# Queries, keys and values kept in DRAM in the layout of their later loads, and the left half of the first output tile moved up to the last GELU

## The chip, the cores and the metric

The kernel runs on one core of one Trainium2 chip. The metric is the device time of one execution in microseconds. Five engines run their own instruction streams: TensorE (PE) multiplies, VectorE (DVE) and ScalarE (ACT) do the elementwise work, GpSimd (POOL) some of it, and the SyncE queue (SP) issues nearly all transfers. Sixteen DMA engines carry the transfers.

## What is computed

One pre-norm layer on x of shape 2048 x 1024 in float32: a token mixer with eight attention heads of width 64 (with forget gates) beside a gated MLP over chunks of 128 positions, one output projection, a dense SwiGLU layer, and a last RMS norm.

```
xn = rms_norm(x, mix_norm_g)
q, k, v, f_logit, z = split(xn @ w_in)                  # 512, 512, 512, 8, 1024 columns
c = cumsum(log_sigmoid(f_logit + b_f))
attn = softmax(q k^T / 8 + c[t] - c[s], s <= t) @ v     # 8 heads of width 64
zu, zv = split(gelu(z)); sgu = zu * (w_s @ layer_norm(zv) + b_s)
x = x + concat(rms_norm(attn), rms_norm(sgu)) @ w_out
gate, up = split(rms_norm(x) @ w_gate_up)
x = x + (silu(gate) * up) @ w_down
out = rms_norm(x)
```

## The kernel before

All products are done in a float32 form with fewer mantissa bits (`F32R`). To keep the accuracy each operand is split into a rounded half ("hi", written h) and the rest ("lo", written l), and a product is the sum of three: hi by hi, hi by lo, lo by hi. A product of 128 x 512 outputs over 1024 inputs is thus 24 matmuls.

**Stage 1, to about 340 us: projections.** The 2048 positions are taken in four chunks of 512 (`c` in line 485). For each chunk the loop at line 508 makes eight products, four for the queries and four for the keys; each holds two heads of 64 rows on the 128 partitions. VectorE scales the result into `ql` (line 521), ScalarE rounds it into `qh` (523 or 528), VectorE leaves the rest in `ql` (524 or 529), and both go to DRAM, 256 KB each (lines 525, 526, 530, 531): `QH`, `QL`, `KH`, `KL`, one tensor of [128, 512] per pair of heads and chunk. `qh` and `ql` are two tiles deep (line 518: pool `p1`, bufs=2), so the tiles of product n+2 are free when the stores of product n have landed. Four products for the values follow (line 557; in the first chunk they come earlier), which `v_close` (419) splits and stores in `VD`. Between the products, `between` (403) lets side work run: the next chunk's loads and splits (`Chunk.steps`), the forget gates (`forget_rows`, which stores f in `FD` and loads it again at line 292 with the block index in front: 4 blocks by 8 heads by 128), and `max_stream` (359), which reads keys and queries back (tiles `A` and `D`) to find the maximum of each row of logits.

All of these transfers stand in one SyncE queue and are issued in order.

**Stage 2, about 340 to 900 us: attention and gates.** `load_keys` (611) brings a block of keys and values: hi and lo of the keys into the two halves of tile `C`, hi again into `D`, and the values in three transfers into `V` (hi, lo, and one column of lo), beside a column of ones that was set once (600 to 604). `prep` (645) does the same for queries (`A`, `B`). `qk` (669) and `pv_of` (706) do the attention steps; ScalarE's exponentials (680) stand between them. In their gaps `z_proj` (815) makes the gates' products, with two transfers of 512 KB for each tile `xz`, and ends each group of four with one GELU over 128 x 2048 (835).

**Output tiles, from about 896 us.** `out_prep` (984) makes the operands of an output tile, `out_tiles` (1060) does its two products (left and right half, `fh` 0 and 1), 24 matmuls each, at line 1079, and adds them to the tile of x. From about 1105 us the SwiGLU layer follows, to the end.

The order on each engine is not that of the code: a scheduler in the build places instructions, and a change in one place moves others by a few places.

Of the kernel before, what the change touches and what calls it, by code (L numbers as in the profile page):

```python
# [15 lines left out]
P = 128  # L16
S = 2048
D = 1024
KT = D // P
# [59 lines left out]
def trunk(ctx: ExitStack, tc: tile.TileContext, x, x_t, mix_g, w_in, b_f, ln_g, ln_b, w_st, b_st, on_g, w_out,  # L79
# [279 lines left out]
    def max_stream(units, pl, ps, pp, nd, ahead):  # L359

        jobs = [(h, j, s) for h, j in units for s in range(j + 1)]
        As, Ds = {}, {}

        def get(n):
            if n < len(jobs):
                h, j, s = jobs[n]
                pr, o = h // 2, (h % 2) * DH
                if s == 0:
                    A = As[h, j] = T(pl, [66, CH], F32R, "A", bufs=2)
                    ldr(A[0:64], QH[pr][j][o : o + DH])  # L370
                    ldr(A[64:66], CR[0:2])
                Dt = Ds[n] = T(pl, [66, CH], F32R, "D", bufs=nd)
                ldr(Dt[0:64], KH[pr][s][o : o + DH])
                ldr(Dt[64:66].rearrange("r (b t) -> r b t", t=P), aug_rows(h, s, slice(2 * j, 2 * j + 2)))

        def turn():
            max_rows(pp, T(ps, [P, 4, P], F32, "mx_ps" if ps is ps2_[0] else "tp", **kw), *late)

        late, kw = None, {"bufs": NMX} if ps is ps2_[0] else {}
        for n in range(ahead):  # L380
            get(n)
        if ps is ps2_[0]:
            yield
        for n, (h, j, s) in enumerate(jobs):
            get(n + ahead)
            if s == 0:
                mx = T(pp, [P, 4, 4], F32, "mx")
            for a in range(4):
                one_max(ps, pp, a, j, s, As[h, j][:, a * P : (a + 1) * P], Ds[n], mx)
                yield  # L390
                if a == 2 and late is not None:
                    turn()
                    late = None
            if s == j:
                late = (h, j, max_split(pp, j, mx))
        yield
        turn()
        yield
# [20 lines left out]
    def v_close(pm, xc, tt):  # L419
        v = T(p1, [P, H, P], F32R, "v") if xc.c else T(p1, [P, H, P], F32R, "xh", bufs=4)  # L420
# [64 lines left out]
    for c in range(NCH):  # L485
# [22 lines left out]
        for which, w in ((0, wq), (1, wk)):  # L508
            for pr in range(4):
# [86 lines left out]

# [3 lines left out]
    with tc.high_priority():  # L600
        for v in vt[:2]:
            nc.vector.memset(f(v[:, :, DH : DH + 1]), 1.0)
    for v in vt[2:]:
        nc.gpsimd.memset(f(v[:, :, DH : DH + 1]), 1.0)
# [6 lines left out]
    def load_keys(h, s, i):  # L611
# [4 lines left out]
        ldr(C[0:64], KH[pr][s][o : o + DH])  # L616
        ldr(C[64:128], KL[pr][s][o : o + DH])
        ldr(Dt[0:64], KH[pr][s][o : o + DH])
        ldr(Dt[64:74].rearrange("r (b t) -> r b t", t=P), aug_rows(h, s, slice(0, 10)))
        vd = VD[s][h].rearrange("(b p) d -> p b d", p=P)  # L620
# [24 lines left out]
    def prep(h, j, res):  # L645
        pr, o = h // 2, (h % 2) * DH
        A = T(p2k, [74, CH], F32R, "A")
        ldr(A[0:64], QH[pr][j][o : o + DH])
        ldr(A[64:72], CR[8 * j : 8 * j + 8])
        B = T(p2k, [P, CH], F32R, "B")  # L650
        ldr(B[0:64], QL[pr][j][o : o + DH])
        ldr(B[64:128], QH[pr][j][o : o + DH])
# [331 lines left out]
    def out_prep(t, o, space=None):  # L984
# [23 lines left out]
        def inputs():  # L1008
            o["x"] = x_tile(t)
            ld(o["x"], x[t * P : (t + 1) * P, :])  # L1010
# [14 lines left out]
        if space is not None:  # L1025
            o["ahead"] = True
# [32 lines left out]

    def out_tiles():  # L1060
        groups = [[0, 1]] + [[t] for t in range(2, NB - 2)] + [[NB - 2, NB - 1]]
        gens = first + [out_prep(t, o[t]) for t in range(2, NB)]
        for its in groups:
# [7 lines left out]
            for fh in range(2):  # L1071
                for t in its:
                    ps = E["bank"]()
                    n = 0
                    for k in (4, 5, 6, 7, 0, 1, 2, 3):
                        wh, wl = (a[:, k % 4, :] for a in o[t]["s"][k // 4])
                        rh, rl = (a[:, k, :] for a in WO[fh])
                        for a, b in ((wh, rh), (wh, rl), (wl, rh)):
                            nc.tensor.matmul(ps, a, b, start=n == 0, stop=n == 3 * KT - 1)
                            n += 1  # L1080
# [41 lines left out]
    for n in range(len(steps) + DEPTH):  # L1122
# [25 lines left out]
        if z_done == z_total and not wg:  # L1148
            while next(zg) == "on":
                pass  # L1150
            for _ in lm:
                pass
            while not all(o[t].get("ahead") for t in range(2)):
                for g in first:
                    next(g)
# [429 lines left out]
```

## Time and profile before

| what | value |
|---|---|
| median of three runs | 2421.05 us (2418.85 to 2423.35) |
| the profiled execution's own time | 2428.99 us |
| its span in the profile | 2427.1 us |
| PE busy | 2369.9 us, 98% |
| VectorE, ScalarE, GpSimd busy | 69%, 44%, 25% |
| DMA | 404920 packets, 372.09 MB, mean 153 GB/s |
| HBM read, written | 249.09 MB, 120.92 MB |

The profile is of one execution. Busy shares are means over stages that are limited by different things; a matmul's busy time overlaps that of the next, so that the pitch from start to start, not the mean duration, is what a matmul costs. "DMA share" is the mean busy share of the 16 DMA engines: a transfer that keeps two of them busy shows as 0.13, one that keeps all of them busy as 1.00. "PEclk" is the share of full speed at which TensorE's clock was granted.

### The profile page before, as it was taken

How to read it: one execution, taken by the hardware profiler on the slowest of the kernel's cores; microseconds unless marked ns; L12 is line 12 of the kernel's file. 1: busy time of each engine (PE TensorE's matmuls, PEld its weight loads, DVE VectorE, ACT ScalarE, POOL GpSimd, SP SyncE). 2: the span in 40 equal slices, each digit the busy share in tenths (PEclk: the TensorE clock that was granted, in tenths of full speed). 3: DMA queues.
4: the chain of work that ended last, by engine and by line, in shares of the span. 5: the costliest groups of instructions: out<-in, count | busy, mean ns of one | idle time of the engine just before them, and what ended most of it. 6: DMA issues, size and time to landing. Idle time of an engine off the chain costs nothing. (4 is left out here: it accounts for less than half of the span.)

```text
span 2427.1 us, 31390 instructions
## 1 busy us (share of the span) xinstructions
PE 2369.9 (98%) x10585; PEld 1902.6 (78%) x10585; DVE 1667.1 (69%) x2710; ACT 1059.1 (44%) x1770; POOL 610.3 (25%) x662
## 2 busy tenths in 40 slices
PE   9999999999999989999999999999999999999997
PEld 7778777777777767787888888788888878888886
DVE  6557677878887666466656555965655596686878
ACT  5322136767777765344333232433323242332333
POOL 1000001121111221221323232332323244363451
PEclk9999999999999989999999999999999999999998
DMA  8856466666686664675432322433232245455443
GB/s 277 298 168 205 127 198 174 172 168 156 156 222 185 183 181 135 200 220 167 122 96 84 91 70 87 139 87 95 76 90 70 87 139 181 166 182 201 160 170 146
DMA packets 404920, 372.09 MB, mean 153 GB/s; under 512 B 72660, under 2 KB 326420, under 8 KB 402712
## 3 DMA queue, kind: packets, MB, share of 16 engines
q1 hardware_dynamic: 399512, 355.33, 48.4%
q0 software_dynamic: 2880, 10.49, 1.5%
q10 hardware_dynamic: 2368, 4.26, 0.5%
q8 instruction: 85, 1.39, 0.2%
q14 instruction: 75, 0.61, 0.1%
HBM read 249.09 MB, written 120.92 MB: 152 GB/s over the span
## 5 line engine op out<-in xcount | busy, mean ns | idle before, releaser
L111 ACT CAST wh<-raw 128x512 fp32r<-128x512 f32 (+2 forms) x496 | 304.3, 620 | 743.9 <-PE pp L1523 620.5
L114 DVE TENSOR_TENSOR wl<-raw,wh 128x512 fp32r<-128x512 f32 (+2 forms) x496 | 371.9, 760 | 87.7 <-ACT wh L111 87.5
L1523 PE MATMUL pp<-wl,wh 128*128 128x512 f32 x1056 | 326.5, 390 | 1.8 <-ACT u L1279 1.0
L1523 PE MATMUL pp<-wh,wh 128*128 128x512 f32 x1056 | 326.1, 390 | 0.0
L1213 POOL TENSOR_TENSOR raw<-raw 128x512 f32<-128x512 f32 (+1 forms) x124 | 169.6, 1369 | 509.7 <-DMA raw<-in_w_gu_dram 351.4
L114 DVE TENSOR_TENSOR Pl<-Pt,Ph 128x512 fp32r<-128x512 f32 (+1 forms) x320 | 195.2, 615 | 87.1 <-ACT Ph L111 82.2
L1523 PEld LDWEIGHTS pp<-wl,wh 128*128 128x128 f32 x1056 | 198.0, 188 | 44.7 <-ACT u L1279 1.4
L1523 PEld LDWEIGHTS pp<-wh,wh 128*128 128x128 f32 x1056 | 198.3, 188 | 41.9
L680 ACT ACTIVATE Pt<-st 128x512 f32<-128x512 f32 (+1 forms) x320 | 169.9, 534 | 136.5 <-PE st L678 132.5
L1523 PE MATMUL pp<-wl,wl 128*128 128x512 f32 x528 | 206.2, 391 | 0.7 <-DVE wl L114 0.7
L1523 PE MATMUL pp<-wh,wl 128*128 128x512 f32 x528 | 206.1, 390 | 0.4 <-DVE wl L114 0.4
L827 PE MATMUL z<-wh,xz 128*128 128x512 f32 x512 | 197.8, 404 | 7.2 <-DMA xz<-XS 7.2
L111 ACT CAST Ph<-Pt 128x512 fp32r<-128x512 f32 (+1 forms) x320 | 176.1, 556 | 27.7 <-PE pv L712 9.1
L1213 DVE TENSOR_TENSOR raw<-raw,raw 128x512 f32<-128x512 f32 (+1 forms) x112 | 133.2, 1192 | 78.9 <-POOL raw L1213 75.5
L335 DVE TENSOR_REDUCE mx<-mx_ps 128x1 f32<-128x512 f32 x192 | 129.8, 683 | 30.5 <-PE mx_ps L333 29.6
L690 POOL TENSOR_SCALAR_AFFINE_SELECT Ph<-Ph 128x128 fp32r<-128x128 f32 x128 | 49.7, 388 | 360.9 <-DVE Pl L114 283.0
L677 PE MATMUL st<-A,D 74*128 74x512 f32 (+1 forms) x320 | 120.4, 376 | 7.2 <-ACT Pt L680 7.0
L710 PE MATMUL pv<-Ph,V 128*128 128x512 f32 (+1 forms) x320 | 120.9, 378 | 4.7 <-POOL Ph L690 3.6
L715 PE MATMUL pv<-Pl,V 128*128 128x512 f32 (+1 forms) x320 | 120.7, 377 | 2.6 <-DVE Pl L114 1.8
L333 PE MATMUL mx_ps<-D,A 66*128 66x512 f32 (+2 forms) x320 | 117.8, 381 | 4.5 <-DMA D<-KH 3.7
L827 PEld LDWEIGHTS z<-wh,xz 128*128 128x128 f32 x512 | 97.7, 192 | 30.0 <-DMA xz<-XS 8.3
L678 PE MATMUL st<-B,C 128*128 128x512 f32 (+1 forms) x320 | 119.5, 374 | 0.0
(315 smaller groups left out, 5295.0 us busy)
## 6 DMA issues: line engine op xcount, KB each, us to landing
raw<-in_w_gu_dram SPq DMA_DIRECT2D x88, 512.0 KB
xz<-XS SPq DMA_DIRECT2D x64, 512.0 KB
HD<-hT SPq DMA_DIRECT2D x44, 512.0 KB
D<-KH SPq DMA_DIRECT2D x112, 128.0 KB
XA<-xa SPq DMA_DIRECT2D x27, 512.0 KB
raw<-HD SPq DMA_DIRECT2D x24, 512.0 KB
XA<-xb SPq DMA_DIRECT2D x21, 512.0 KB
xa<-XA SPq DMA_DIRECT2D x20, 512.0 KB
```

Of the source, the lines that this page charges most:

```text
L111: return nc.scalar.copy(o, i) if eng is nc.scalar else eng.tensor_copy(o, i)
L114: return eng.tensor_tensor(o, i, f(h), ALU.subtract)
L333: nc.tensor.matmul(pm[:, 0:n], lhs, Dt[0 : lhs.shape[0], 0:n], start=True, stop=True)
L335: nc.vector.tensor_reduce(mx[:, a, s : s + 1], pm, AX.X, ALU.max)
L677: nc.tensor.matmul(st[:, off:], Dt[:, b * P : (b + 1) * P], A[:, off:], start=True, stop=False)
L678: nc.tensor.matmul(st[:, off:], C[:, b * P : (b + 1) * P], B[:, off:], start=False, stop=True)
L680: nc.scalar.activation(Pt[:, off:], st[:, off:], AF.Exp)
L710: nc.tensor.matmul(pv[:, off:], V[:, 0:P], Ph[:, off:], start=kb == 0, stop=False)
L715: nc.tensor.matmul(pv[:, off:], V[:, 0:P], Pl[:, off:], start=False, stop=kb == 4 * j + 3)
L827: nc.tensor.matmul(pz, xz[:, a, k, :], w[b][:, k, :], start=n == 0, stop=n == 3 * KT - 1)
L1213: (nc.vector if e == "v" else nc.gpsimd).tensor_tensor(o, a, b, op)
L1523: nc.tensor.matmul(pm, a[:, k, :], b[:, k, :], start=on is None and k == 0 and e == 0, stop=k == it.kh - 1 and e == 2, skip_group_check=n ...
```

## The change

There are two parts.

**Layout in DRAM.** `QH` and `QL` become one tensor `QC`, `KH` and `KL` one tensor `KC`, of shape [2, 2, 64, 512]: head of the pair, half (queries: lo then hi; keys: hi then lo), row, position. What a block of attention needs, hi and lo of one head, now lies in one piece of 128 rows, and tiles `C` and `B` are loaded with one transfer each where there were two. The stores of `qh` and `ql` each go to `[:, 0]` or `[:, 1]` of that tensor: two pieces of 64 rows that lie 65,536 elements apart. `VD` gets a row of 129 numbers (hi, one, lo without its first column, that column), so that `V` is loaded with one transfer of 128 x 4 x 129 where there were three. For that `v_close` has GpSimd set the ones and VectorE write the lo half in two pieces, and the setting of the ones in `V` falls away. `xz` is loaded with one transfer of 1 MB.

**First output tile.** The operands of tile 0 are split ahead of the end of the gates into a free `zr` tile; behind the last GELU the 24 matmuls of its left half run into a bank of the gates' pool, VectorE adds them to the left half of x (`x0`), and `out_tiles` leaves them out. ScalarE copies `x0` into the tile of x when that tile exists.

```
-    QH = [[T(dram, [P, CH], F32R, f"QH{p}_{c}") for c in range(NCH)] for p in range(4)]
-    QL = [[T(dram, [P, CH], F32R, f"QL{p}_{c}") for c in range(NCH)] for p in range(4)]
-    KH = [[T(dram, [P, CH], F32R, f"KH{p}_{c}") for c in range(NCH)] for p in range(4)]
-    KL = [[T(dram, [P, CH], F32R, f"KL{p}_{c}") for c in range(NCH)] for p in range(4)]
-    VD = [T(dram, [H, CH, P], F32R, f"VD{c}") for c in range(NCH)]
+    QC = [[T(dram, [2, 2, DH, CH], F32R, f"QC{p}_{c}") for c in range(NCH)] for p in range(4)]
+    KC = [[T(dram, [2, 2, DH, CH], F32R, f"KC{p}_{c}") for c in range(NCH)] for p in range(4)]
+    VD = [T(dram, [H, CH, P + 1], F32R, f"VD{c}") for c in range(NCH)]
...
+        nc.gpsimd.memset(f(v[:, :, DH : DH + 1]), 1.0)
         a = nc.scalar.activation(v[:, :, 0:DH], pmv, AF.Copy, scale=r)
-        b = nc.vector.scalar_tensor_tensor(v[:, :, DH:P], pmv, r, f(v[:, :, 0:DH]), ALU.mult, ALU.subtract)
+        nc.vector.scalar_tensor_tensor(v[:, :, P : P + 1], pmv[:, :, 0:1], r, f(v[:, :, 0:1]), ALU.mult, ALU.subtract)
+        b = nc.vector.scalar_tensor_tensor(v[:, :, DH + 1 : P], pmv[:, :, 1:DH], r, f(v[:, :, 1:DH]), ALU.mult, ALU.subtract)
...
-                    ldr(QH[pr][c], qh)
-                    ldr(QL[pr][c], ql)
+                    ldr(QC[pr][c][:, 1], qh)
+                    ldr(QC[pr][c][:, 0], ql)
...
-                    ldr(KH[pr][c], qh)
-                    ldr(KL[pr][c], ql)
+                    ldr(KC[pr][c][:, 0], qh)
+                    ldr(KC[pr][c][:, 1], ql)
...
-        ldr(C[0:64], KH[pr][s][o : o + DH])
-        ldr(C[64:128], KL[pr][s][o : o + DH])
-        ldr(Dt[0:64], KH[pr][s][o : o + DH])
+        ldr(C, KC[pr][s][h % 2].rearrange("a d t -> (a d) t"))
+        ldr(Dt[0:64], KC[pr][s][h % 2, 0])
...
-        ldr(V[:, :, 0:DH], vd[:, :, 0:DH])
-        ldr(V[:, :, DH + 1 : P], vd[:, :, DH + 1 : P])
-        ldr(V[:, :, P : P + 1], vd[:, :, DH : DH + 1])
+        ldr(V, VD[s][h].rearrange("(b p) d -> p b d", p=P))
...
-            for a in range(2):
-                ldr(xz[:, a], XS[q][:, a, :, cc * P : (cc + 1) * P])
+            ldr(xz.rearrange("p a k t -> p (a k) t"),
+                XS[q][:, :, :, cc * P : (cc + 1) * P].rearrange("p a k t -> p (a k) t"))
...
+            if t == 0:
+                ld(x0, x[0:P, 0:CH])
+                early = T(p2z, [P, 4, 4, P], F32R, "zr", bufs=2)
+                for i, part in enumerate((at, r[:, 4:8, :])):
+                    hi_of(nc.scalar, early[:, 2 * i], part)
+                    lo_of(nc.vector, early[:, 2 * i + 1], part, early[:, 2 * i])
...
+            pz = T(psz, [P, CH], F32, "z", bufs=NZ)
+            for kt in K_OUT:
+                out_product(pz, 0, 0, kt)
+            nc.vector.tensor_tensor(x0, x0, pz, ALU.add)
```

Two places of the order are what the prediction speaks of. First the SyncE queue in the second chunk of stage 1, before the change, from the stores of one query product to those of the next (`XS`: copy of the normalised x; `xt`: a load of x for the next chunk; `A`, `D`: operands of `max_stream`).

```order
L108 DMA QH_1_16_79<-qh_1016 128x512
L108 DMA QL_1_32_95<-ql_1017 128x512
L108 DMA XS_9_72<-xh_910 128x1024
L108 DMA XS_9_72<-xl_914 128x1024
L234 DMA xt_1031<-in_x_t_dram 128x2x512
L108 DMA A_1042<-QH_0_15_78 64x512
L108 DMA A_1042<-CR_231 2x512
L108 DMA D_1045<-KH_0_47_110 64x512
L108 DMA D_1045<-AUG_146 2x4x128
L108 DMA QH_1_20_83<-qh_1082 128x512
L108 DMA QL_1_36_99<-ql_1083 128x512
```

The same place of the same queue with the change.

```order
L108 DMA QC_1_16_79<-qh_992 2x64x512
L108 DMA QC_1_16_79<-ql_993 2x64x512
L108 DMA XS_9_72<-xh_886 128x1024
L108 DMA XS_9_72<-xl_890 128x1024
L233 DMA xt_1007<-in_x_t_dram 128x2x512
L108 DMA A_1018<-QC_0_15_78 64x512
L108 DMA A_1018<-CR_199 2x512
L108 DMA D_1021<-KC_0_31_94 64x512
L108 DMA D_1021<-AUG_114 2x4x128
L108 DMA QC_1_20_83<-qh_1058 2x64x512
L108 DMA QC_1_20_83<-ql_1059 2x64x512
```

The order of the transfers is the same; the DRAM side of the four stores is now 2 by 64 by 512 where it was 128 by 512.

Second TensorE behind the last GELU, before the change (`pv`, `st`: the attention's products; the last rows of the old step and the first of the new one).

```order
L710 MATMUL pv_9859<-Ph_9915,V_847_3341 128x512
L712 MATMUL pv_9859<-Ph_9915,V_847_3341 1x512
L715 MATMUL pv_9859<-Pl_9917,V_847_3341 128x512
L677 MATMUL st_10027<-A_9391,D_860_3361 128x512
L678 MATMUL st_10027<-B_9394,C_855_3356 128x512
```

And with the change (`z_9778`: the bank of the gates' pool; `wh`, `wl` on its right: the output weights; `zr_9661`: the split operands of tile 0).

```order
L702 MATMUL pv_9710<-Ph_9730,V_815_3341 128x512
L704 MATMUL pv_9710<-Ph_9730,V_815_3341 1x512
L707 MATMUL pv_9710<-Pl_9732,V_815_3341 128x512
L1069 MATMUL z_9778<-wh_6988,zr_9661 128x512
L1069 MATMUL z_9778<-wl_6989,zr_9661 128x512
...
L669 MATMUL st_9832<-A_9244,D_829_3357 128x512
L670 MATMUL st_9832<-B_9247,C_824_3352 128x512
```

The 24 matmuls of the tile's left half now stand between the two attention steps; before the change they were the first 24 of the group that starts at line 1079.

More of the change, by code (lines that the diff above doesn't have):

```diff
@@ L419, in v_close @@
     def v_close(pm, xc, tt):
-        v = T(p1, [P, H, P], F32R, "v") if xc.c else T(p1, [P, H, P], F32R, "xh", bufs=4)
+        v = T(p1, [P, H, P + 1], F32R, "v") if xc.c else T(p1, [P, H, P + 1], F32R, "xh", bufs=4)
         r = r1[:, xc.c * 4 + tt : xc.c * 4 + tt + 1]
         pmv = pm.rearrange("p (h d) -> p h d", h=H)
+        nc.gpsimd.memset(f(v[:, :, DH : DH + 1]), 1.0)
         a = nc.scalar.activation(v[:, :, 0:DH], pmv, AF.Copy, scale=r)
-        b = nc.vector.scalar_tensor_tensor(v[:, :, DH:P], pmv, r, f(v[:, :, 0:DH]), ALU.mult, ALU.subtract)
+        nc.vector.scalar_tensor_tensor(v[:, :, P : P + 1], pmv[:, :, 0:1], r, f(v[:, :, 0:1]), ALU.mult, ALU.subtract)
+        b = nc.vector.scalar_tensor_tensor(v[:, :, DH + 1 : P], pmv[:, :, 1:DH], r, f(v[:, :, 1:DH]), ALU.mult, ALU.subtract)
         s = ldr(VD[xc.c][:, tt * P : (tt + 1) * P, :].rearrange("h p d -> p h d"), v)
@@ L599, in trunk @@
     m0 = T(p2, [P, 1], F32, "m0", bufs=1)
[L600 to L604, printed above, removed]
+    x0 = T(p2, [P, CH], F32, "x0", bufs=1)
     nc.vector.memset(f(one_r), 1.0)
@@ L647, in prep @@
         A = T(p2k, [74, CH], F32R, "A")
-        ldr(A[0:64], QH[pr][j][o : o + DH])
+        ldr(A[0:64], QC[pr][j][h % 2, 1])
         ldr(A[64:72], CR[8 * j : 8 * j + 8])
         B = T(p2k, [P, CH], F32R, "B")
-        ldr(B[0:64], QL[pr][j][o : o + DH])
-        ldr(B[64:128], QH[pr][j][o : o + DH])
+        ldr(B, QC[pr][j][h % 2].rearrange("a d t -> (a d) t"))
         res[h, j] = (A, B)
@@ L1009, in inputs @@
             o["x"] = x_tile(t)
-            ld(o["x"], x[t * P : (t + 1) * P, :])
+            if t == 0:
+                ld(o["x"][:, CH:], x[0:P, CH:])
+                nc.scalar.copy(o["x"][:, 0:CH], x0)
+            else:
+                ld(o["x"], x[t * P : (t + 1) * P, :])
         if space is None:
@@ L1025, in out_prep @@
         if space is not None:
+            if t == 0:
+                ld(x0, x[0:P, 0:CH])
[3 more added lines that the diff above has]
+                    lo_of(nc.vector, early[:, 2 * i + 1], part, early[:, 2 * i])
+                o["s"] = [(early[:, 2 * i], early[:, 2 * i + 1]) for i in range(2)]
             o["ahead"] = True
@@ L1058, in trunk, with out_product @@
     posts = []
+    K_OUT = (4, 5, 6, 7, 0, 1, 2, 3)
+    def out_product(ps, t, fh, k):
+        wh, wl = (a[:, k % 4, :] for a in o[t]["s"][k // 4])
+        rh, rl = (a[:, k, :] for a in WO[fh])
+        for e, (a, b) in enumerate(((wh, rh), (wh, rl), (wl, rh))):
+            nc.tensor.matmul(ps, a, b, start=k == K_OUT[0] and e == 0, stop=k == K_OUT[-1] and e == 2)
     def out_tiles():
@@ L1072, in out_tiles @@
                 for t in its:
+                    if t == fh == 0:
+                        continue
                     ps = E["bank"]()
[L1074 to L1080, printed above, removed]
+                    for k in K_OUT:
+                        out_product(ps, t, fh, k)
                         if k % 2 == 1:
```

6 lines of the change are left out of this document (3 added, 3 removed).

## The prediction

> **What bounds the kernel now.** I read the page first, then the waits of TensorE, then a table of stage 1 by its parts, then single transfers in the SyncE queue, and last the place of the last GELU.
>
> ```profile
> span 2427.1 us, 31390 instructions
> PE   9999999999999989999999999999999999999997
> DMA  8856466666686664675432322433232245455443
> ...
> PE z L827 <- DMA xz<-XS: 7.2, 6, 2.9
> PE st L677 <- ACT Pt L680: 7.0, 2, 6.5
> ```
>
> TensorE is the bound: its row is 9 nearly everywhere, and its longest waits come to 7 us each in all. So a change can win little by taking waits away, some 15 us, and can lose whatever it puts in TensorE's way. The DMA row says where that is most likely: its first six slices of 61 us, which is stage 1, are the fullest stretch. Here is stage 1 by its parts; query and key products (first, second, fourth, sixth row) alternate with value products and gates.
>
> ```profile
> core 0: us, PE busy (x) PEld busy (x) DVE busy (x) ACT busy (x) POOL busy (x), PEclk, DMA share, GB/s
> 43.00:97.00 54.00, 50.78 (x228) 39.68 (x228) 29.81 (x52) 22.00 (x32) 3.98 (x5) 1.00 0.84 312
> 97.00:150.00 53.00, 52.63 (x241) 41.44 (x239) 34.52 (x103) 18.09 (x26) 1.04 (x1) 1.00 0.66 226
> 150.00:177.00 27.00, 27.00 (x121) 19.84 (x120) 12.79 (x43) 3.37 (x5) 0.00 (x0) 1.00 0.55 158
> 177.00:239.00 62.00, 62.00 (x285) 50.00 (x284) 49.24 (x132) 19.55 (x28) 1.01 (x1) 1.00 0.62 201
> 239.00:264.00 25.00, 25.00 (x112) 17.94 (x111) 16.83 (x50) 2.73 (x5) 0.00 (x0) 1.00 0.60 172
> 264.00:323.00 59.00, 58.30 (x257) 46.31 (x256) 45.72 (x110) 11.88 (x17) 1.48 (x2) 1.00 0.42 134
> 323.00:340.00 17.00, 17.00 (x76) 13.45 (x76) 10.77 (x26) 3.92 (x5) 1.64 (x5) 1.00 0.87 251
> ```
>
> TensorE is busy in 292.7 of these 297 us. The DMA engines are busy too: duration by share, 45.4 + 35.0 + 14.9 + 38.4 + 15.0 + 24.8 + 14.8, makes 188 us for the average engine. The cover is there, but only because the load is spread over all sixteen.
>
> **The stores of queries and keys: on how many engines?** This is the step on which everything hangs. Before, a store is 128 rows on both sides; now its DRAM side is 2 pieces of 64 rows. The trace holds two transfers whose leading count is not a multiple of 16: the load of `jk`, 34 rows, and that of `F`, whose DRAM side starts with the 4 blocks (line 292) while its tile has 32 rows. Here are the queue around both, and the DMA share while the packets of each were moving; the last row is a full store of 128 rows.
>
> ```profile
> 40.44 0.25 SPq L209 DMA_DIRECT2D jk<-in_c_row_dram  x1
> 43.26 0.33 SPq L108 DMA_DIRECT2D QH<-qh  x1
> ...
> 175.27 0.69 SPq L292 DMA_DIRECT2D F<-FD  x1
> 176.06 0.48 SPq L108 DMA_DIRECT2D A<-QH  x1
> ```
>
> ```profile
> 176.80:177.03 0.23, 0.23 (x2) 0.19 (x1) 0.21 (x1) 0.00 (x0) 0.00 (x0) 1.00 0.17 51
> 176.93:177.03 0.10, 0.10 (x2) 0.06 (x1) 0.08 (x1) 0.00 (x0) 0.00 (x0) 1.00 0.22 67
> ...
> 43.25:44.05 0.80, 0.80 (x5) 0.64 (x4) 0.69 (x1) 0.80 (x1) 0.00 (x0) 1.00 0.13 51
> 44.25:44.60 0.35, 0.35 (x3) 0.31 (x2) 0.35 (x1) 0.35 (x1) 0.00 (x0) 1.00 1.03 392
> ```
>
> The 34 rows moved at a share of 0.13, two engines of sixteen (2 is the largest number up to 16 that divides 34). `F` moved at 0.17 to 0.22, three to four engines, though its tile has 32 rows: the side with the smaller leading count, 4, decided. The full store ran on all, at 392 GB/s. By these rows a side of 2 by 64 by 512 leaves two engines for each of the new stores. What speaks against: in `F` the small count is on the side that is read, in the new stores on the side that is written.
>
> [...]
>
> **What that costs.** The number and size of these stores:
>
> ```profile
> QH<-qh SPq DMA_DIRECT2D x16, 256.0 KB
> QL<-ql SPq DMA_DIRECT2D x16, 256.0 KB
> KH<-qh SPq DMA_DIRECT2D x16, 256.0 KB
> KL<-ql SPq DMA_DIRECT2D x16, 256.0 KB
> ```
>
> - Before: 64 x 262,144 bytes are 16.8 MB; at 392 GB/s over all engines 43 us of each engine's 188. Everything else is 145 us per engine.
> - Now the two engines carry 64 stores one behind the other. At the 51 GB/s of the two-engine row a store takes 5.14 us; at an eighth of 392 GB/s 5.35 us. In all 329 to 342 us.
> - The other transfers still use these two engines for their share: 145 us. Sum 474 to 487 us of work for two engines, in a stage that lasted 297. All stand in one queue, and per product the pair of stores (10.3 us) and the rest (145 / 32 = 4.5) make 14.8 us against 24 matmuls at 27.00 / 121 = 0.223 us, 5.4 us, with side work 6.7 us (54 / 8). So the two engines become the bound of stage 1, TensorE waits for `ql` to come free, and the stage lasts 177 to 190 us longer. I take 180.
> - Lower bound: the transfers of the last row (0.87 x 17 = 15 us) can run behind the last key store, and the rest may move faster with fourteen engines idle (312 / 0.84 = 371 GB/s against 392, 5%, 7 us): 329 + 145 - 22 = 452, 155 us longer. Upper bound: in value products and gates (27 + 25 + 17 = 69 us) no query or key is stored; if the two engines run dry there, 190 + 69 = 259 us longer. I stay near the lower end, since two products' tiles (2 x 14.8 us) are still waiting to be stored when the value products (about 27 us) begin, so the engines have work through nearly all of them.
>
> **Around it.** 32 loads of `C` and of `B` fall to one from two, `V` to one from three, `xz` to one from two: 160 transfers less in the SyncE queue, where none was the bound; at most the 7.2 us of waits for `xz` can go with them, and since the first matmul now waits for 1 MB instead of 512 KB, they can also grow by as much. The memsets on GpSimd and the split lo in `v_close` lie on engines that are idle for half of the stage or, now, wait with TensorE.
>
> **The last GELU.** ScalarE's order there, TensorE behind it, and the clock in the windows around it and around an earlier wait for `xz`:
>
> ```profile
> 873.76 1.28 ACT L835 ACT_TABLE_LOAD   x1
> 875.05 1.91 ACT L835 ACTIVATE zr<-zr 128x2048 f32<-128x2048 f32 x1
> 876.87 2.16 ACT L111 CAST wh<-raw 128x512 fp32r<-128x512 f32 x4
> ...
> 880.97 0.60 ACT L680 ACTIVATE Pt<-st 128x512 f32<-128x512 f32 x1
> ```
>
> ```profile
> 881.62 0.80 PE L677 MATMUL st<-A,D 74*128 74x512 f32 x1 [6.54 <-ACT Pt L680]
> ...
> 883.82 0.63 PE L715 MATMUL pv<-Pl,V 128*128 128x512 f32 x1
> 884.25 0.63 PE L678 MATMUL st<-B,C 128*128 128x512 f32 x1
> ```
>
> ```profile
> 853.90:857.00 3.10, 1.48 (x6) 0.99 0.68 179
> 857.00:863.80 6.80, 6.77 (x19) 0.50 0.00 0
> ...
> 881.60:887.70 6.10, 6.08 (x13) 0.50 0.66 217
> ```
>
> TensorE stands for 6.54 us because the exponential waits behind a table load, the GELU and four casts. Then it runs at half clock: 0.43 us from start to start instead of 0.22, so that the 6.1 us hold about 3 us of loss. The 24 matmuls moved here (24 x 0.223 = 5.4 us) fill the hole, and the clock need not fall: 5.4 + 3 = 8.4 us, at least 5.4 if the clock falls all the same, 0 if their operands come late. With up to 7 us either way from `xz` and the half clock after it (19 matmuls in 6.8 us, 2.6 us lost), I take 10 us for all gains, between 0 and 18.
>
> **The sum.** Against the profiled execution, whose 2428.99 us are 1.9 above its span: 2429 + 180 - 10 = 2599 us. That execution lies 7.9 us above the median of the runs (2421.05), so 2591 us for a median. With the bounds: 2421 + 155 - 18 = 2558, and 2421 + 259 - 0 = 2680. What 0.2% is here, 4.8 us, is about what a measurement can tell from no change.
>
> **Rivals.**
> - The stores keep all sixteen engines (the tile's 128 rows decide when the tile is read). Then stage 1 stays as it is, bound by TensorE, and only the gains remain: 2421 - 10 = 2411 us, faster; 2421 if they fail. For it: in neither of the two transfers is the small count on the written side alone. Against it: `F` used four engines though its tile allowed sixteen. It decides at the first query store, about 43 us: a share of 1.0 or of 0.13. Chance 0.11.
> - Two engines, and nothing to overlap. The `D` and `A` loads stand behind the stores in one queue; if TensorE is held by them so that each pair of stores is waited for with no product under it, stage 1 is the old 297 us plus all 329: 2421 + 329 - 10 = 2740 us. It decides when TensorE's lead over the stores falls below one product. Against it: `D` is loaded a job or more ahead, and 6.7 us of products stand against 14.8 of transfers. For it: the clock. After a wait with 1.48 us of work in 3.1, the clock was 0.50 in the next 6.8 us; in a stage where TensorE works less than half of the time a product may cost 24 x 0.43 = 10.3 us, and with side work at the same clock about 13 of the 14.8, so that the cover is nearly gone. Chance 0.09.
>
> [...] With the clock at full speed throughout I would give this rival 0.05.
>
> **How the numbers follow.** Two engines with overlap: 0.80, forecast 2591 us, own range 2558 to 2680. The range for 8 in 10 leaves out the first rival and the far part of the second and widens the own range a little to both sides for the unknown spread of the load over the engines: 2545 to 2700 us. Faster by over 0.2%: 0.09, the first rival with its gains; the same: 0.02, that rival without them; slower: 0.89.
>
> **What would show it.** In the profile after: a DMA share near 0.13 in stretches of stage 1, with waits of VectorE at line 521's operation (or of TensorE behind it) for the stores; the first attention product at about 340 + 180 = 520 us instead of 340; stage 2 about as long as before; no wait of 6.5 us at the last GELU. A stage 1 that still ends near 340 us makes the forecast wrong by its largest term; one that ends beyond 600 us says that nothing overlapped.

## The result

| | time, us | against the kernel before |
|---|---|---|
| forecast | 2591 (2545 to 2700) | +170 |
| kernel before | 2419.95 median (2416.37 to 2423.35, 4 runs) | |
| changed kernel | 2631.48 median (2623.29 to 2633.68, 4 runs) | +211.5; ratio 1.0868, 95% interval 1.0839 to 1.0897 |

The page of the changed kernel, the rows that answer to those of before, with the clock, and TensorE's two longest waits:

```profile
span 2631.9 us, 31312 instructions
PE   8546778679999999899999999999999999999998
PEclk9768888879999999999999999999999999999998
DMA  8423534277555667557653232333323325456353
...
PE mx_ps L332 <- DMA D<-AUG: 100.0, 17, 33.9
PE tp L306 <- DVE v L302: 24.1, 2, 21.5
```

All that is new lies in the first nine slices (a slice is now 66 us). There TensorE was at 9 and is at 4 to 8, and the DMA row, which was at 4 to 8, is at 2 to 5 in seven of the nine: TensorE works less *and* the DMA engines are busy for a smaller share. That is what few full engines beside idle ones would look like. Here is the stage (the first row is all of it), then a stretch of 10 us in it, in the columns of the windows above:

```profile
43.00:546.00 503.00, 343.11 (x1310) 260.89 (x1310) 202.14 (x518) 81.60 (x116) 10.02 (x21) 0.82 0.41 123
...
43.00:100.00 57.00, 28.64 (x120) 22.79 (x119) 19.25 (x31) 15.62 (x22) 2.94 (x4) 0.78 0.64 205
100.00:147.00 47.00, 38.62 (x151) 29.23 (x151) 10.19 (x20) 6.14 (x9) 1.10 (x2) 0.86 0.33 118
147.00:194.00 47.00, 13.89 (x49) 10.67 (x50) 16.46 (x45) 10.56 (x16) 0.11 (x1) 0.57 0.33 105
...
423.00:546.00 123.00, 90.15 (x344) 69.12 (x343) 57.15 (x136) 15.15 (x21) 3.15 (x6) 0.85 0.32 94
...
150.00:160.00 10.00, 0.00 (x0) 0.00 (x0) 1.38 (x2) 0.63 (x1) 0.00 (x0) 0.50 0.13 51
```

The last row shows it bare: TensorE does nothing for 10 us, the share is 0.13, two of sixteen, at 51 GB/s, to the digit what the 34 rows of `jk` moved at. In the stage as a whole TensorE is busy for 343.1 us where it was 292.7, with the same number of matmuls (1310 and 1309): the 50 us more go with the lower clock (0.82 where it was 1.00). It is idle for 160 us where it was 4.

Three landmarks, as rows of the timeline: the first attention product, the first product of the gates' `z`, and the last one. Before:

```profile
339.85 0.40 PE L677 MATMUL st<-A,D 74*128 74x512 f32 x1
...
350.37 0.63 PE L827 MATMUL z<-wh,xz 128*128 128x512 f32 x1
...
871.88 0.40 PE L827 MATMUL z<-wh,xz 128*128 128x512 f32 x1
```

And in the changed kernel the first two, with the two holes between them:

```profile
545.98 0.40 PE L669 MATMUL st<-A,D 74*128 74x512 f32 x1
...
554.93 0.58 PE L669 MATMUL st<-A,D 74*128 74x256 f32 x1 [7.97 <-ACT Pt L672]
...
563.33 1.19 PE L332 MATMUL mx_ps<-D,A 66*128 66x512 f32 x2 [7.28 <-DMA D<-AUG]
...
568.91 0.63 PE L819 MATMUL z<-wh,xz 128*128 128x512 f32 x1
```

The first attention product comes 206.1 us later, the first product of `z` 218.5 us later: the handover to stage 2 has lost another 12.4 us. From there on the changed kernel's trace is the shorter one. The windows from the first `z` to the last and from there to the end, before and after:

```profile
350.00:872.00 522.00, 510.78 (x2402) 399.15 (x2401) 406.55 (x800) 384.30 (x694) 100.05 (x246) 0.99 0.65 174
872.00:2427.00 1555.00, 1520.12 (x6694) 1239.80 (x6692) 1031.63 (x1351) 566.95 (x922) 493.69 (x385) 0.99 0.42 132
```

```profile
569.00:1083.00 514.00, 506.82 (x2398) 397.74 (x2397) 407.70 (x802) 383.73 (x695) 99.00 (x246) 0.99 0.62 175
1083.00:2632.00 1549.00, 1518.84 (x6693) 1238.26 (x6691) 1027.67 (x1351) 566.69 (x922) 494.87 (x385) 0.99 0.42 133
```

522 became 514 and 1555 became 1549, about 14 us less. So 218.5 - 14 = 205 us, which is the difference of the two spans (2631.9 - 2427.1). Not all of the 14 us is a gain: the profiled execution before took 2428.99 us, 9 us more than the median of its runs. Three kernels of the next section that keep the old loads (all stores changed, half of them, two queues) took 515.0, 516.4 and 513.7 us for the stretch from the first `z` to the last (two more, with halves in one queue and TensorE's program in another order, 532 and 535), so the changed kernel's 514 us there shows next to no gain. At the last GELU the wait of 6.54 us has shrunk to 0.94:

```profile
1092.42 0.50 PE L669 MATMUL st<-A,D 74*128 74x512 f32 x1 [0.94 <-ACT Pt L672]
```

### The profile page after: what moved, and what is told of

It reads as the page before. It is cut to its first block, busy times and chain, and to the rows that moved or that the text cites. A ratio compares the mean times of both kernels' runs of the same rounds, so it can differ in the third digit from the quotient of the medians.

```text
span 2631.9 us, 31312 instructions
## 1 busy us (share of the span) xinstructions
PE 2416.6 (92%) x10585; PEld 1933.3 (73%) x10585; DVE 1668.3 (63%) x2726; ACT 1060.0 (40%) x1773; POOL 611.9 (23%) x675
## 5 line engine op out<-in xcount | busy, mean ns | idle before, releaser
L332 PE MATMUL mx_ps<-D,A 66*128 66x512 f32 (+2 forms) x320 | 129.4, 417 | 115.0 <-DMA D<-AUG 100.0
L1536 PE MATMUL pp<-wh,wl 128*128 128x512 f32 x528 | 206.1, 390 | 0.0
L332 PEld LDWEIGHTS mx_ps<-D,A 66*128 66x128 f32 x320 | 66.2, 211 | 142.5 <-issue 45.9
```

Of the source, the lines that this page charges most:

```text
L332: nc.tensor.matmul(pm[:, 0:n], lhs, Dt[0 : lhs.shape[0], 0:n], start=True, stop=True)
L1536: nc.tensor.matmul(pm, a[:, k, :], b[:, k, :], start=on is None and k == 0 and e == 0, stop=k == it.kh - 1 and e == 2, skip_group_check=n ...
```

## The experiments

The theory: the stores, split over a side of two pieces, run on two DMA engines, and stage 1 lasts as long as these two have work. The rivals: the new values' path did it; the order of one queue did it; or each such store costs a wait of its own. Each kernel ran in a round beside the kernel before, whose median was 2421.86 us (only the stores, the two with interleaved rows and whole value rows, the changed kernel with halved stores), 2421.27 (half of the stores, own queue, old values, halves in the kernel before), 2423.06 (layout with old values and without the tile, wide rows, even and odd rows) and 2423.42 (two queues). Medians of different rounds are compared below as they are, so a difference between them is sure to about 2 us only.

**Only the stores, in the kernel before.** `QH`, `QL`, `KH` and `KL` become two pieces of 65 rows, of which 64 are used, so that the two can't be read as one run of 128 rows. Nothing else is touched.

```diff
-    QH = [[T(dram, [P, CH], F32R, f"QH{p}_{c}") ...
+    QH = [[T(dram, [2, DH + 1, CH], F32R, f"QH{p}_{c}") ...
-                    ldr(QH[pr][c], qh)
+                    ldr(QH[pr][c][:, 0:DH], qh)
```

> The kernel before, with one thing changed: QH, QL, KH and KL are [2, 65, 512] tensors of which 64 rows each are used, so that a store's DRAM side is 2 by 64 by 512; the loads still read 64 contiguous rows. Theory (two engines per store, the small count on the written side decides as well): stage 1 lasts about 205 us longer as in the changed kernel, 2620 to 2650 us. Rival (the values' path, or any other part of the change): no difference, 2420 us.

Measured: 2619.16 us (2617.33 to 2621.09), ratio 1.0816, interval 1.0802 to 1.083. Its first attention product and first `z` product, its stage 1 and TensorE's longest wait there:

```profile
532.55 0.40 PE L677 MATMUL st<-A,D 74*128 74x512 f32 x1
...
548.43 0.40 PE L827 MATMUL z<-wh,xz 128*128 128x512 f32 x1
```

```profile
43.00:532.00 489.00, 343.98 (x1305) 262.68 (x1304) 202.41 (x510) 81.25 (x115) 9.14 (x14) 0.82 0.37 122
```

```profile
PE mx_ps L333 <- DMA D<-AUG: 85.2, 16, 33.0
```

+197 us from the shape of the stores' targets alone, with the old values' path; the same wait and the same clock as in the changed kernel. That is 0.8 us below the range expected. The rival of the values' path falls.

**Only half of the stores.** The same for `QL` and `KL` alone.

```diff
-    QL = [[T(dram, [P, CH], F32R, f"QL{p}_{c}") ...
+    QL = [[T(dram, [2, DH + 1, CH], F32R, f"QL{p}_{c}") ...
-                    ldr(QL[pr][c], ql)
+                    ldr(QL[pr][c][:, 0:DH], ql)
```

> The kernel before, with only the 32 stores of the rounded-off parts (ql) going to a target of two pieces; the 32 of qh stay whole. Theory (two engines have to move these stores, and the stage lasts as long as their work): 32 x 5.3 us + (188 - 32 x 0.67) us = 337 us against 297 us, so about 2460 us, 2450 to 2485, with the first attention product near 380 to 400 us. Rival (each such store costs a wait of its own, whatever the engines have left): half of what all 64 cost, 197 / 2 = 99 us, so about 2520 us and the first product near 440 us.

Measured: 2480.78 us (2479.45 to 2483.58), ratio 1.0247, interval 1.0229 to 1.0266: +59.5 us, at the upper end of the theory's range and far from the rival's 99.

```profile
396.14 0.40 PE L677 MATMUL st<-A,D 74*128 74x512 f32 x1
```

```profile
PE mx_ps L333 <- DMA D<-AUG: 29.8, 7, 12.7
```

Half of the stores cost 30% of what all of them do, and TensorE's longest wait is a third as long: the first part of the two engines' work is hidden under TensorE's 297 us, and only what goes beyond shows. That is a sum of work against a cover, not a price per store. From 43 us the stage lasted 353 us where the sum gave 337; what filled the 16 us between is not shown.

**The stores in a queue of their own.** The changed kernel, its 64 stores issued by ScalarE.

```diff
-                    ldr(QC[pr][c][:, 1], qh)
+                    nc.scalar.dma_start(f(QC[pr][c][:, 1]), f(qh))
```

(and so for the other three)

> The changed kernel, with the 64 two-piece stores issued by ScalarE into its own queue, so that the D and A loads of the maximum pass no longer stand behind them in SyncE's queue. Theory (the work of two engines is the bound): the loads still need the same two engines, so the stage stays within 155 to 220 us of the old one: 2575 to 2640 us. Rival (the order in one queue is what holds TensorE): most of it comes back, under 2480 us.

Measured: 2619.47 us (2617.37 to 2622.62), ratio 1.082, interval 1.08 to 1.0839.

```profile
536.94 0.40 PE L669 MATMUL st<-A,D 74*128 74x512 f32 x1
```

```profile
PE mx_ps L332 <- DVE mx L337: 50.2, 11, 13.3
PE mx_ps L332 <- DVE mx L334: 24.3, 5, 7.4
PE mx_ps L332 <- DMA D<-AUG: 17.7, 3, 8.1
```

The wait for `D` falls from 100 to 18 us, and the time hardly at all (12 us): TensorE now waits for VectorE, which in turn waits for the stores to free `ql` (41.4 us for those of `QC`, 40.5 for those of `KC`). With another issuer the time is nearly the same (2619 us against 2631), so the order of the one queue did not make the loss. The line that the wait named, the load of `D`, was where the shortage surfaced, not what caused it.

**The layout with its rows interleaved.** Now the remedy: `QC` and `KC` as [head, row, half, position]. The DRAM side of a store is then 128 rows that lie 4 KB apart, and a head's operand is still one contiguous piece of DRAM, with hi and lo rows alternating in `B` and `C` alike (the sum over the 128 rows is the same up to its order).

```diff
-    QC = [[T(dram, [2, 2, DH, CH], F32R, ...
+    QC = [[T(dram, [2, DH, 2, CH], F32R, ...
-                    ldr(QC[pr][c][:, 1], qh)
+                    ldr(QC[pr][c][:, :, 1].rearrange("h d t -> (h d) t"), qh)
-        ldr(B, QC[pr][j][h % 2].rearrange("a d t -> (a d) t"))
+        ldr(B, QC[pr][j][h % 2].rearrange("d a t -> (d a) t"))
```

> The changed kernel with QC and KC in the order head, row, half, position: a store has 128 rows 4 KB apart on its DRAM side, the load of C or B is one contiguous piece of 128 rows in which hi and lo alternate by partition (in C and B alike, so that the sum over partitions is the same). Theory: stores and loads both run on sixteen engines, one transfer each; 2405 to 2412 us, equal to the kernel with two transfers per store or some us less. Rival (the values' path): near 2630 us.

Measured: 2422.73 us (2418.06 to 2426.57), ratio 1.0001, interval 0.9992 to 1.001. The loss is gone, which shows the cause from the other side. But the gain of some 10 us that was expected with it is missing, here and in the same kernel without the output tile:

> The interleaved layout without the part on the first output tile: loads in one transfer, stores over sixteen engines, tile 0 in its old place. Theory: the hole at the last GELU, 6.5 us and some 3 us of half clock, is back, so 5 to 9 us more than the interleaved kernel with the tile moved: 2412 to 2420 us, against 2420 before. If the moved tile is worth nothing, the two are within 2 us of each other.

Measured: 2428.29 us (2425.61 to 2432.63), ratio 1.0032, interval 1.0022 to 1.0043. Both expectations missed on the same side, so something else in the two kernels costs time. The timeline of the one with the tile has it in stage 1, with a wait at `tp` (TensorE's transposes) that was 1.8 us before; the last row is the kernel before:

```profile
347.13 0.40 PE L669 MATMUL st<-A,D 74*128 74x512 f32 x1
...
362.25 0.47 PE L819 MATMUL z<-wh,xz 128*128 128x512 f32 x1
```

```profile
PE tp L306 <- DVE v L302: 5.7, 2, 5.4
...
PE tp L307 <- DVE v L303: 1.8, 2, 1.2
```

The stage ends 7.3 us late, at a DMA share of 0.70 where the kernel before had 0.64. The first stretch in which only the values' path differs is 28 to 43 us, where the first `VD` stores run. That window in the kernel before and in the one with interleaved rows:

```profile
28.00:43.00 15.00, 15.00 (x69) 11.15 (x68) 5.40 (x8) 4.78 (x8) 0.31 (x1) 1.00 0.59 181
```

```profile
28.00:43.00 15.00, 15.00 (x69) 11.17 (x68) 5.84 (x12) 5.51 (x9) 0.00 (x0) 1.00 0.88 117
```

The engines are half as busy again (0.88 for 0.59) and move a third less. By the packet records from 43 us to the first attention product, a packet of 512 bytes (nearly all are value rows) takes 28.8 ns on the mean in the kernel before and one of 516 bytes 48.9 ns in this kernel. The prediction had this edit at no cost.

**The values' path as before.** The interleaved layout and the moved tile, but with rows of 512 bytes in `VD`, three loads of `V` and the ones set in the tile.

```diff
-    VD = [T(dram, [H, CH, P + 1], F32R, f"VD{c}") for c in range(NCH)]
+    VD = [T(dram, [H, CH, P], F32R, f"VD{c}") for c in range(NCH)]
-        ldr(V, VD[s][h].rearrange("(b p) d -> p b d", p=P))
+        vd = VD[s][h].rearrange("(b p) d -> p b d", p=P)
+        ldr(V[:, :, 0:DH], vd[:, :, 0:DH])
+        ldr(V[:, :, DH + 1 : P], vd[:, :, DH + 1 : P])
+        ldr(V[:, :, P : P + 1], vd[:, :, DH : DH + 1])
```

> The interleaved layout (one transfer per operand, all 16 engines) and the output tile moved, but the values' path as before: rows of 512 bytes in DRAM, three loads of V, the ones set in the tile. Theory (the rows of 516 bytes cost about 7 us in stage 1 and one V load instead of three gains nothing): 2411 to 2417 us, 5 to 11 us below the kernel with the interleaved layout and whole V rows (2422.7), first attention product back near 340 us. Rival (the single V load is what shortens the attention and z part by about 12 us): that gain goes as well, 2420 to 2430 us.

Measured: 2408.1 us (2406.09 to 2411.14), ratio 0.9946, interval 0.993 to 0.9963. This beats both kernels, by 13 us and by 223 us.

```profile
338.26 0.39 PE L674 MATMUL st<-A,D 74*128 74x512 f32 x1
...
350.05 0.40 PE L824 MATMUL z<-wh,xz 128*128 128x512 f32 x1
```

```profile
350.00:859.00 509.00, 502.74 (x2391) 394.55 (x2391) 406.90 (x802) 382.57 (x694) 99.05 (x246) 1.00 0.65 177
859.00:2407.00 1548.00, 1518.47 (x6695) 1239.04 (x6693) 1029.09 (x1351) 567.00 (x923) 495.12 (x385) 0.99 0.42 133
```

The values' path costs 2422.7 - 2408.1 = 14.6 us, twice what the first attention product had shown (8.9 us of it before that product, 3.3 between it and the first `z`). The stretch of `z` takes 509 us with three loads of `V`, and 510 in the kernel with one (362.25 to 872.03 us), so the single load of `V` was not what shortened it: that rival falls. The time came out 3 us below the range.

**The same without the tile.**

> The interleaved layout with the values' path as before, and without the moved output tile. If the tile is worth what it was with the whole V rows (2428.3 - 2422.7 = 5.6 us), this is 2408.1 + 5.6 = 2413.7 us, 2411 to 2417, and the layout alone gains 5 to 10 us. Rival (the 13 us of the kernel with both are nearly all the tile's, 8.4 us and what it triggers): 2417 to 2422 us.

Measured: 2415.81 us (2413.99 to 2419.5), ratio 0.9971, interval 0.996 to 0.9982. The interleaved layout with old value rows gains 7.2 us, the tile 2415.8 - 2408.1 = 7.7 us more (5.9 when each of the two is taken against the kernel before of its own round; 5.6 with the 516-byte rows). Without the tile the wait at the last GELU is back:

```profile
871.14 0.79 PE L673 MATMUL st<-A,D 74*128 74x512 f32 x1 [6.54 <-ACT Pt L676]
```

**Is it the size of the row or where it starts?** The interleaved kernel again with rows of 516 bytes, one load of `V`, but a row every 1024 bytes.

```diff
-    VD = [T(dram, [H, CH, P + 1], F32R, f"VD{c}") for c in range(NCH)]
+    VD = [T(dram, [H, CH, 2 * P], F32R, f"VD{c}") for c in range(NCH)]
```

(stores and loads take columns 0 to 128 of it)

> The interleaved layout with the tile moved and whole V rows of 129 numbers (516 bytes), which start every 1024 bytes in DRAM instead of every 516. Theory A (a row of 516 bytes costs more whatever its start): as with the rows packed, 2419 to 2426 us. Theory B (it is rows that start at odd places): near the kernel with rows of 512 bytes, 2406 to 2413 us, first attention product back from 347 to about 339 us.

Measured: 2413.43 us (2409.35 to 2418.18), ratio 0.9961, interval 0.9948 to 0.9974.

```profile
342.32 0.40 PE L669 MATMUL st<-A,D 74*128 74x512 f32 x1
```

```profile
28.00:43.00 15.00, 15.00 (x69) 11.18 (x68) 5.79 (x12) 5.48 (x9) 0.00 (x0) 1.00 0.83 140
```

Of the 14.6 us, 9.3 go with the pitch of 1024 bytes in place of 516 and 5.3 stay: between the two theories, nearer to the second. The mean packet of 516 bytes falls from 48.9 to 31.1 ns. Why the wider pitch costs less no run shows. In the stretch from 28 us, where the stores come thick, 140 GB/s are still less than the 181 of 512-byte rows, and a packet takes 49.1 ns there (62.0 with packed rows, 26.5 with 512 bytes). What makes the part that stays is open: the length of the row, its start in the tile (still every 516 bytes), or the rest of the values' path (memset on GpSimd, lo in two pieces, one load of `V`), which no run undid alone.

**Halved stores: a miss, and its cause.** The first try at a remedy was to leave the changed kernel's layout and split each store into two of 64 rows, each with 64 as its leading count on both sides.

```diff
-                    ldr(QC[pr][c][:, 1], qh)
+                    for hh in range(2):
+                        ldr(QC[pr][c][hh, 1], qh[hh * DH : (hh + 1) * DH])
```

> The changed kernel with each store of qh and ql issued as two transfers of 64 rows, each into one contiguous piece of 64 by 512; all else as changed. Theory (a store whose DRAM side leads with 2 runs on two of the sixteen engines, and these two engines are the bound of stage 1): 64 rows can be spread over sixteen engines, the first attention product comes back to 340 to 345 us, and the time is 2405 to 2415 us, a little under the kernel before; 64 more issues of 0.3 us in the SyncE queue cost nothing. Rival (the values' path made stage 1 long: GpSimd's memset waits 160 us for stores of VD, rows of 516 bytes, lo written in two pieces): nothing of that is undone here, so the time stays near 2630 us.

Measured: 2467.48 us (2463.93 to 2477.53), ratio 1.0196, interval 1.0178 to 1.0214. Most of the loss is gone, but the kernel is 46 us slower than before, where 7 to 17 us faster was expected. The first suspicion was the half of the partitions. Two kernels put it to the test in the kernel before, with old targets: halves,

```diff
-                    ldr(QH[pr][c], qh)
+                    for hh in range(2):
+                        ldr(QH[pr][c][hh * DH : (hh + 1) * DH], qh[hh * DH : (hh + 1) * DH])
```

> The kernel before, with each of the 64 stores of Q and K issued as two transfers of 64 partitions, targets and everything else as they were. Theory A (transfers from half of the partitions are what made the changed kernel with halved stores end stage 1 at 384 us): most of that comes here too, 2450 to 2470 us, first attention product at 370 to 385 us. Theory B (halving is free, and it was the new targets or the value rows): 2419 to 2426 us, first product within 5 us of 340.

and even and odd rows (`[hh::2]` on both sides):

> The kernel before, with each of the 64 stores of Q and K issued as two transfers again, but of its even and its odd rows, so that each reads from all over the 128 partitions. Theory A (64 neighbouring partitions feed a transfer more slowly than 128 do, which made the kernel with halved stores 57 us slower): 2420 to 2435 us, first attention product near 340 us. Theory B (it is the number of transfers, 64 more in SyncE's queue, or their half size): as with halves, 2465 to 2490 us.

Measured: 2478.58 us (2475.26 to 2484.72), ratio 1.024 (1.0218 to 1.0261), and 2475.28 us (2472.84 to 2482.47), ratio 1.0221 (1.0204 to 1.0238). The second takes rows from all partitions and loses as much, so the suspicion falls. The records say so as well: a packet of 2048 bytes took 125 ns in stage 1 with halves and 98 ns with even and odd rows (100 before), and the time is the same. What the two have in common is the program. Counting along TensorE's program, so many weight products (`mm`) stand ahead of the 23rd, 43rd and 83rd product of the maximum pass:

```
                             23rd  43rd  83rd
before                        538   675   867
changed kernel                541   677   860
halved, SyncE (three kernels) 619   764 to 765   950 to 952
halved, SyncE and ScalarE     538   673   867
```

With 64 transfers more in the SyncE queue the build placed TensorE's instructions otherwise, and the maximum pass later. The last row is the kernel that tells size from program: the second half of each store goes out through ScalarE.

```diff
-                    ldr(QH[pr][c], qh)
+                    ldr(QH[pr][c][0:DH], qh[0:DH])
+                    nc.scalar.dma_start(f(QH[pr][c][DH:P]), f(qh[DH:P]))
```

> The kernel before, with each of the 64 stores of Q and K halved into 64 rows each as before, but the second half issued by ScalarE into its own queue. The program's order is then that of the kernel before (391, 557 and 822 weight products stand ahead of the 16th, 36th and 76th maximum product, against 391, 557 and 822 before and 452, 642 and 912 with both halves in SyncE's queue). Theory (the later place of the maximum products, or the 64 more transfers in SyncE's queue, cost the 52 to 57 us): 2418 to 2432 us, first attention product at 338 to 346 us. Rival (transfers of half the size cost it, whoever issues them): 2465 to 2485 us.

(The counts in this text take in all products on the maximum pass's banks from the 21st on; the table above counts those of the pass alone.)

Measured: 2424.51 us (2422.44 to 2431.19), ratio 1.0011, interval 1.0001 to 1.0022. Here is the stage from 54 to 340 us in the kernel before, with the halves in one queue, and with the halves in two:

```profile
54.00:340.00 286.00, 281.71 (x1261) 219.63 (x1261) 191.74 (x501) 75.65 (x110) 6.93 (x11) 1.00 0.63 206
```

```profile
54.00:340.00 286.00, 261.26 (x1109) 198.73 (x1108) 159.84 (x418) 65.06 (x97) 3.81 (x4) 0.95 0.60 177
```

```profile
54.00:340.00 286.00, 276.62 (x1219) 214.93 (x1218) 191.96 (x492) 77.75 (x111) 6.74 (x8) 0.98 0.64 198
```

With the halves in one queue TensorE gets through 1109 matmuls in that time, with two queues through 1219, before through 1261. Its first attention product still comes 3 us later than the range said, but the time is within it:

```profile
348.97 0.39 PE L681 MATMUL st<-A,D 74*128 74x512 f32 x1
```

So neither the size of the transfers nor the partitions cost the 46 to 57 us. They come with 64 more transfers in SyncE's queue and the program that goes with them. Which of these two it is, the later place of the maximum pass or the queue itself, stays open, since both went back together. In any case the first remedy's miss tells nothing about 64-row transfers as such.

## Why the prediction was right, and where its sizes were off

**The bound and the place.** Right in the main: TensorE bounds the kernel, and what was lost was lost in stage 1 and the handover behind it. The reading that stage 1 is the fullest stretch of the DMA row was not: the mean share is 0.66 in the first six slices and 0.66 in the next six, and only the rate is higher (212 GB/s against 175). Nothing in the sum hangs on it; stage 1 lost because the 64 stores stand there.

**Two engines for the new stores.** Right, in the open point too: the small count stood on the written side alone, and it still decided (the kernel with only the stores changed, +197 us; 0.13 at 51 GB/s in a stretch of the trace). The leading counts read so far are 2 and 34 (a share of 0.13 each), 4 (0.17 to 0.22) and 128 (1.03); what rule joins them no run tests. The rival with sixteen engines (2411 us) is out by this. Its time, though, is what the kernel with interleaved rows and old values reached, 2408 us: there stage 1 runs at a share of 0.64 and 211 GB/s, as before (0.64 and 209).

**What that costs: +180 us, 155 to 259.** The mechanism held and the size was somewhat low. The sum was 474 to 487 us of work for two engines; the kernel with only the stores changed needed 489.5 us from 43 us to its first attention product (532.5), which is 192.7 us more than before, plus 5.4 us in the handover (548.4 - 532.5 = 15.9 us against 10.5). So the plain sum, +177 to 190, was right within 3 us up to that product, and the two engines hardly ran dry. An estimate says the same: a share of 0.37 over 489 us is 181 us for the average engine, of which the stores make 2 x 329 / 16 = 41; if the other 140 are spread evenly over the sixteen, the two had about 329 + 140 = 469 us of work. The reason given for staying at the lower end (tiles of two products still waiting) fits this; no run tests it by itself. The kernel with half of the stores fits the same sum within 16 us.

**The second rival, no overlap, 2740 us.** Its point was a lower clock in the waits. The clock did fall, to 0.82 over the stage, and TensorE's busy time grew by 50 us. But this cost nearly nothing before the first attention product: TensorE was the one that waited, 343 us of busy time fit into stages of 489 and 503 us, and the first of these is close to what the two engines' work alone had given (474 to 487).

**"Around it": at no cost.** This is the term that failed. The prediction looked at the engines that make the values (memsets, the split lo) and at the number of transfers. It did not ask what a row of 516 bytes at odd places costs the DMA engines. Measured: 14.6 us for the whole values' path in the interleaved layout, of which 9.3 go with the pitch of 516 bytes in DRAM. In the changed kernel the first attention product comes 13.4 us later than in the kernel with only the stores changed (546.0 against 532.5). The `xz` part of this term went to the good side: the waits of `z` for `xz`, 7.2 us before, no longer show in the changed kernel or in the best one. In the five kernels with interleaved rows the stretch of `z` takes 508 to 511 us, where the three with the old loads took 514 to 516; in the changed kernel itself it takes 514. How much of this is `xz` no run separates.

**The last GELU: -8.4 us, at least -5.4.** Measured -7.7 (-5.9 by rounds) and -5.6, between two pairs of kernels that differ in the tile alone. The wait of 6.54 us became 0.94.

**All gains: -10 us, between 0 and -18.** Measured 13.2 us in all in the best kernel. In the changed kernel the part behind the first `z` product is 5.3 us shorter than in the kernel with only the stores changed (2063.0 us against 2068.3), and that is about what the tile alone is worth.

**The sum.** Measured piece by piece: +197 for the stores, +14.6 for the value rows, -13 for the gains, together +199 us. The changed kernel lost 211.5. The 12 us between are not settled by a run, but the traces say roughly where they lie. Against the kernel with only the stores changed, the changed kernel's first `z` product comes 20.5 us later (568.9 us against 548.4), where the value rows cost 8.9 + 3.3 = 12.2 us in the interleaved layout. And from there to the end it gains 5.3 us, where the best kernel gains 11.2 (2057.1 us against 2068.3). That two costs on the same two engines make more than their sum would explain the first; this was only argued. Why the second gain is smaller stays open.

**Luck.** The forecast of +170 us was 41 us too low, and the measured time lies inside the range all the same. The range had been opened upward for two engines that run dry in the value products, which hardly happened. That this room also covered the value rows and the 12 us was luck; the mechanism and the main term were not.

The prediction of a first attention product at 520 us was low by 26; its marks (a share of 0.13, waits of VectorE for the stores at the operation that makes `ql`, no long wait at the GELU) were all there. The second of them, in the waits of VectorE:

```profile
DVE ql L523 <- DMA KC<-ql: 66.4, 9, 9.9
DVE ql L523 <- DMA QC<-ql: 45.7, 8, 9.0
```

In the kernel before, the same operation's wait was for TensorE:

```profile
DVE ql L521 <- PE mm L516: 23.4, 9, 3.5
```

## What to carry to other kernels

Before changing a layout for the sake of a later load, look at what each *store* becomes: here the leading count of its DRAM side, 2, left two of sixteen engines to carry it (a share of 0.13), and an order of dimensions, [head, row, half] for [head, half, row], gave the same contiguous load without the loss (2422.7 us against 2631.5). Count work per engine, not per kernel: with two engines full, the mean DMA share of stage 1 went down, from 0.64 to 0.41, while the transfers became the bound. And a layout that saves two transfers by making a row four bytes longer may be paid for with every row: here 48.9 ns per packet against 28.8, 14.6 us for the whole values' path, and no gain to be seen from the single load.

## What the runs showed of the hardware that was not expected

- Rows of 516 bytes packed one behind the other: 48.9 ns per packet from 43 us to the end of stage 1 against 28.8 ns for 512 bytes; 31.1 ns when each starts at a multiple of 1024 bytes. In the stretch of 15 us with the first such stores 117 GB/s at a share of 0.88, against 181 at 0.59 for 512 bytes and 140 at 0.83 for the wide rows.
- Packets of 2048 bytes (the stores, and loads with rows of that size) took 125 ns in stage 1 when the stores were halves of 64 neighbouring partitions, 98 ns with 64 even or odd ones, 100 ns with all 128; the first two kernels' times differ by 3 us (2478.6 and 2475.3).
- SyncE's issue of a store of `qh` or `ql` took 0.46 us on the mean before and 1.36 us in the changed kernel, up to 6.6 us for one, while the two engines were behind.
- 64 more transfers in SyncE's queue came with another order of TensorE's program and cost 52 to 57 us (46 in all with the changed layout); through a second queue they cost 1.
